# Instance norm of 268 MB on one core: tiles of 48 KiB per partition in four slots, masked sums, and the last stores on the load queue

## Chip, cores, metric

One core of one Trainium2 chip. The metric is the device time of one execution in microseconds; the span in a profile is about 1.7 us shorter. The engines go by the names of the profile: DVE is VectorE, ACT ScalarE, PE TensorE, POOL GpSimd, SP SyncE, which here only issues transfers. The transfers themselves are done by 16 DMA engines; a packet is what one of them moves as one record, here one row of one partition (the 63 whole loads of before, of 128 rows each, are 8,064 packets of 32 KiB) or a 4-byte write to a semaphore.

## The reference

```python
x = np.random.randn(8, 64, 32, 64, 64).astype(np.float32)   # 512 instances of 131072 elements
mean = np.mean(x, axis=(2, 3, 4), keepdims=True)
var = np.var(x, axis=(2, 3, 4), keepdims=True)
return ((x - mean) / np.sqrt(var + eps)).astype(np.float32)
```

268.4 MB are read once and 268.4 MB written once.

## The kernel before

A tile is 4 MB: 8 instances, 16 partitions each, 32 KiB per partition. Six slots (buffers in SBUF, the on-chip memory) hold tiles; SP issues loads, ACT issues stores. DVE and ACT share the sums and the final scaling, and TensorE averages over the partitions of an instance. The last tile is cut into two halves so that the compute after the last load is short.

```python
COLS = 8192
SLOTS = 6
...
def on_vector(eng, t, lane, n, c1, c2, c16):
    w = t.shape[1] // 2
    eng.reduce_sum(out=a[:, 0:1], in_=t[:, :w], ...)        # waits: landed
    ...
    eng.tensor_scalar(out=t[:, w:], ...)                    # (x * scale) + shift
def on_scalar(eng, t, lane, n, c1, c2, c16, dst):
    eng.activation(..., in_=t[:, w:], func=Act.Identity, accum_out=a[:, 1:2])
    eng.activation(..., in_=t, func=Act.Square, bias=a[:, 2:3], accum_out=a[:, 3:4])
    ...
    eng.activation(out=t[:, :w], ..., scale=a[:, 5:6], bias=a[:, 6:7])
    eng.dma_start(out=dst, in_=t)._wait_ge(done[lane], c2).then_inc(stored[lane], 16)
...
def load_all(eng):                                          # on SP
    for s in range(SLOTS):
        eng.dma_start(out=slots[s][:], in_=x_t[s]).then_inc(landed[s], 16)
    ...                                                     # then each load waits for its slot's store
```

## Time and profile before

| | before |
|---|---|
| time, median of the first three runs | 1248.04 us (1247.95 to 1248.22) |
| span of the profiled run | 1246.2 us |
| ACT, DVE busy | 79%, 38% |
| packets of the two data queues, share of 16 DMA engines | 99.9% |
| bytes over the span | 431 GB/s |

Read the queue shares first: they say whether the DMA engines have any time left. The lines are in the prediction below.

### The profile page before, as it was taken

The page shows a single profiled execution, that of the slowest core. Times are in us where ns is not written, and L with a number is a line of the kernel's source. Part 1 is how long each engine was busy: PE and PEld are TensorE (multiplying, and loading weights), DVE is VectorE, ACT ScalarE, POOL GpSimd, SP SyncE. Part 2 cuts the span into 40 slices and gives each one's busy share as a digit, 9 for nine tenths or more (in the row PEclk, how much of TensorE's full clock was granted, in tenths as well). Part 3 has the DMA queues.
Part 4 walks back from the last instruction along what each step waited for, and adds up shares of the span by engine and source line. Part 5 has one row for each costly group of instructions (what it writes and reads, how often), then busy time and mean ns, then how long its engine had stood idle before and what let it go on. Part 6 is the DMA issues. An engine that isn't in the chain of part 4 may idle for free.

```text
span 1246.2 us, 1808 instructions
## 1 busy us (share of the span) xinstructions
PE 76.4 (6%) x260; PEld 65.2 (5%) x260; DVE 468.0 (38%) x325; ACT 986.1 (79%) x410; POOL 1.9 (0%) x11
## 2 busy tenths in 40 slices
PE   0000000000000000000000000000000000000000
PEld 0000000000000000000000000000000000000000
DVE  2344334433334334343343433434334333343331
ACT  5888888887787878778777877787787778878774
POOL 0000000000000000000000000000000000000000
DMA  9999999999999999999999999999999999999998
GB/s 404 421 438 428 430 438 436 428 431 438 435 429 431 438 435 429 431 436 436 429 431 436 436 429 430 438 436 426 433 438 436 426 433 438 435 425 435 438 429 380
DMA packets 18722, 536.90 MB, mean 431 GB/s; under 512 B 2080, under 2 KB 2080, under 8 KB 2080
## 3 DMA queue, kind: packets, MB, share of 16 engines
q1 hardware_dynamic: 9360, 268.44, 50.0%
q10 hardware_dynamic: 9360, 268.44, 49.9%
q14 instruction: 2, 0.02, 0.0%
HBM read 268.44 MB, written 268.44 MB: 431 GB/s over the span
## 4 chain that ended last, share of the span: by engine, by line
ACT 48%; DVE 29%; another core or an unknown queue 13%; PE 6%; issue 1%; DMA 1%; ACTq 0%; DVEq 0%; SPq 0%
ACT unused L113 37%; DVE small L79 18%; DVE slot L95 8%; ACT slot L123 4%; ACT unused L107 4%; PE psum L136 3%; PE psum L143 3%; ACT small L120 1%; ACT L120 1%; DMA slot<-in_x_dram 1%; DVE small L89 1%; DVE small L82 1%; DVE small L92 1%; ACTq L130 0%
## 5 line engine op out<-in xcount | busy, mean ns | idle before, releaser
L113 ACT ACTIVATE unused<-slot,small 128x8192 uint8<-128x8192 f32 (+1 forms) x65 | 456.1, 7016 | 90.2 <-DVE small L82 90.2
L79 DVE TENSOR_REDUCE small<-slot 128x1 f32<-128x4096 f32 (+1 forms) x65 | 283.0, 4353 | 163.7 <-DMA slot<-in_x_dram 163.7
L107 ACT ACTIVATE unused<-slot 128x4096 uint8<-128x4096 f32 (+1 forms) x65 | 231.7, 3564 | 81.9 <-DMA slot<-in_x_dram 76.7
L123 ACT ACTIVATE slot<-slot,small 128x4096 f32<-128x4096 f32 (+1 forms) x65 | 243.7, 3749 | 27.6 <-DVE small L92 27.6
L89 DVE RECIPROCAL small<-small 128x1 f32<-128x1 f32 x65 | 10.6, 164 | 533.8 <-ACT small L120 533.8
L95 DVE TENSOR_SCALAR slot<-slot,small 128x4096 f32<-128x4096 f32 (+1 forms) x65 | 154.7, 2380 | 2.4
L136 PE MATMUL psum<-small,avg 128*128 128x2 f32 x130 | 38.2, 363 | 673.9 <-DVE small L79 548.5
L136 PEld LDWEIGHTS psum<-small,avg 128*128 128x128 f32 x130 | 32.6, 311 | 679.4 <-DVE small L79 552.7
L143 PE MATMUL psum<-small,avg 128*128 128x1 f32 x130 | 38.2, 363 | 480.6 <-ACT unused L113 480.6
L143 PEld LDWEIGHTS psum<-small,avg 128*128 128x128 f32 x130 | 32.7, 312 | 486.1 <-ACT unused L113 486.1
L120 ACT ACTIVATE small<-psum,eps_t 128x1 f32<-128x1 f32 x65 | 17.0, 261 | 37.4 <-PE psum L143 37.3
L82 DVE TENSOR_REDUCE small<-psum 128x1 f32<-128x2 f32 x65 | 10.4, 160 | 62.8 <-PE psum L136 62.8
L107 ACT ACT_TABLE_LOAD x10 | 12.8, 1283 | 10.4 <-ACT slot L123 7.1
L120 ACT ACT_TABLE_LOAD x10 | 12.8, 1283 | 0.2
L107 ACT ACTIVATION_READ_ACCUMULATOR unused<-slot 128x1 f32 x65 | 12.1, 186 | 0.0
L113 ACT ACTIVATION_READ_ACCUMULATOR unused<-slot,small 128x1 f32 x65 | 12.1, 186 | 0.0
L92 DVE TENSOR_TENSOR small<-small 128x1 f32<-128x1 f32 x65 | 10.4, 159 | 2.2
L204 POOL TENSOR_SCALAR_AFFINE_SELECT avg<-avg 128x128 f32<-128x128 f32 x4 | 1.3, 324 | 0.3
L201 POOL MEMSET avg<- 128x128 f32 x2 | 0.4, 204 | 0.5 <-SPq L42 0.5
L246 POOL MEMSET const-bfloat16-1.0<- 128x1 bf16 x1 | 0.1, 101 | 0.0
L246 POOL MEMSET const-uint8-127<- 128x1 uint8 x1 | 0.1, 101 | 0.0
L214 POOL MEMSET eps_t<- 128x1 f32 x1 | 0.1, 99 | 0.0
(2 smaller groups left out, 0.2 us busy)
## 6 DMA issues: line engine op xcount, KB each, us to landing
slot<-in_x_dram SPq DMA_DIRECT2D x63, 4096.0 KB, 53.3
out_dram<-slot ACTq DMA_DIRECT2D x63, 4096.0 KB, 45.3
slot<-in_x_dram SPq DMA_DIRECT2D x2, 2048.0 KB, 55.6
out_dram<-slot ACTq DMA_DIRECT2D x2, 2048.0 KB, 14.7
```

Source lines behind the costliest of these rows:

```text
L79: eng.reduce_sum(out=a[:, 0:1], in_=t[:, :w], axis=mybir.AxisListType.X)._wait_ge(landed[lane], c16).then_inc(summed[lane], 1)
L82: eng.tensor_reduce(out=a[:, 2:3], in_=psum[lane][:, 0:2], axis=mybir.AxisListType.X, op=Alu.add, negate=True,)._wait_ge(meaned[lane], c1) ...
L89: eng.reciprocal(out=a[:, 5:6], in_=a[:, 4:5])._wait_ge(rooted[lane], c1).then_inc(scaled[lane], 1)
L92: eng.tensor_mul(out=a[:, 6:7], in0=a[:, 2:3], in1=a[:, 5:6])._wait_ge(scaled[lane], c1).then_inc(shifted[lane], 1)
L95: eng.tensor_scalar(out=t[:, w:], in0=t[:, w:], scalar1=a[:, 5:6], scalar2=a[:, 6:7], op0=Alu.mult, op1=Alu.add,)._wait_ge(shifted[lane], ...
L107: eng.activation(out=unused[:, w : 2 * w], in_=t[:, w:], func=Act.Identity, accum_out=a[:, 1:2],)._wait_ge(landed[lane], c16).then_inc(sum ...
L113: eng.activation(out=unused[:, : 2 * w], in_=t, func=Act.Square, bias=a[:, 2:3], accum_out=a[:, 3:4],)._wait_ge(centred[lane], c1).then_in ...
L120: eng.activation(out=a[:, 4:5], in_=psum[lane][:, 2:3], func=Act.Sqrt, bias=eps_t[:, 0:1])._wait_ge(varied[lane], c1).then_inc(rooted[lane ...
L123: eng.activation(out=t[:, :w], in_=t[:, :w], func=Act.Identity, scale=a[:, 5:6], bias=a[:, 6:7],)._wait_ge(shifted[lane], c1).then_inc(don ...
L136: eng.matmul(out=psum[lane][:, 0:2], lhsT=avg[n][:], rhs=a[:, 0:2], start=True, stop=True,)._wait_ge(summed[lane], c2).then_inc(meaned[lan ...
L143: eng.matmul(out=psum[lane][:, 2:3], lhsT=avg[n][:], rhs=a[:, 3:4], start=True, stop=True,)._wait_ge(squared[lane], c1).then_inc(varied[la ...
L204: eng.affine_select(out=m[:], in_=m[:], pattern=[[sign * split, n], [0, split]], compare_op=Alu.is_ge, fill=0.0, base=0 if sign < 0 else s ...
```

## The change

Its intent: fewer and longer packets (48 KiB rows instead of 32 KiB), compute that starts after 2 MB instead of 4 MB, and an end in which the last stores come close behind the last loads. A tile of 6 MB holds 12 instances whose borders fall inside a partition's row, so sums are kept by chunk of 16 KiB and put together with masks. Two parts of 2 MB come first, 41 tiles follow, three parts of 2 MB end it. The last whole tile and these three parts are stored by SP, behind the last loads.

```diff
-    COLS = 8192
-    SLOTS = 6
+    CHUNK = 4096
+    THIRDS = 3
+    COLS = THIRDS * CHUNK
+    SLOTS = 4
+    FRONT = 2
+    n_tiles = (n_inst // PART - FRONT) // THIRDS - 1
+    n_parts = n_inst // PART - THIRDS * n_tiles
 ... (layout of tiles and parts, masks, semaphores)
+    def over_instance(eng, a, p, at, m, to, negate, c1, wait, steps):
+        eng.tensor_tensor(...)   # sums by chunk times mask
+        eng.tensor_reduce(...)   # of what TensorE averaged
+        eng.tensor_tensor(...)   # back to chunks
+        eng.tensor_reduce(...)
 ... (DVE squares chunk 0, ACT chunks 1 and 2; DVE scales 0 and 1, ACT 2)
+        for m in range(FRONT, n_parts):
+            part(m)                                   # last three loads
+        eng.dma_start(out=out_t[TAIL], in_=slots[s][:])._wait_ge(done[s], ...)
+        for m in range(FRONT, n_parts):
+            eng.dma_start(out=part_of(out_f, m), in_=t)._wait_ge(done[lane], 2)...
```

## The prediction

"Latencies some 3" is an estimate that the trace of before bears out: twice 1.02 us from the first issue (1.03) to the first packet (2.05) and 0.46 from the end of the last packet (1244.68) to the last landing (1245.14) are 3.0. The times of ACT and DVE that the compute per tile is worked out from are in the last fence.

> **What bounds the kernel now.** I read the page first (busy shares, DMA rows, queues), then the groups by shape, the waits of the engines and of the load queue, and the rates of three stretches.
>
> From the page:
>
> ```profile
> PE 76.4 (6%) x260; PEld 65.2 (5%) x260; DVE 468.0 (38%) x325; ACT 986.1 (79%) x410; POOL 1.9 (0%) x11
> ...
> DMA  9999999999999999999999999999999999999998
> ...
> DMA packets 18722, 536.90 MB, mean 431 GB/s; under 512 B 2080, under 2 KB 2080, under 8 KB 2080
> ...
> q1 hardware_dynamic: 9360, 268.44, 50.0%
> q10 hardware_dynamic: 9360, 268.44, 49.9%
> ...
> slot<-in_x_dram SPq DMA_DIRECT2D x63, 4096.0 KB, 53.3
> out_dram<-slot ACTq DMA_DIRECT2D x63, 4096.0 KB, 45.3
> ```
>
> The two queues' packets fill 99.9% of the time of all 16 DMA engines: there is no hole for better overlap to fill. A 4 MB load needs 53.3 us to land and a store 45.3 us, though 4.19 MB at 431 GB/s is 9.7 us: both queues always hold a backlog. ACT at 79% has room.
>
> The stretches (columns: PE, weight loads, DVE, ACT and POOL busy, clock, DMA share, GB/s) show start, middle and end:
>
> ```profile
> 0.00:3.00 3.00, 0.00 (x0) 0.00 (x0) 0.00 (x0) 0.00 (x0) 1.89 (x11) 1.00 0.65 175
> 3.00:1240.00 1237.00, 76.36 (x260) 65.23 (x260) 468.02 (x325) 986.06 (x410) 0.00 (x0) 1.00 1.00 433
> 1240.00:1246.20 6.20, 0.00 (x0) 0.00 (x0) 0.00 (x0) 0.00 (x0) 0.00 (x0) 1.00 0.43 182
> ```
>
> The middle runs at share 1.00 for 1237 us. What the edges lose is small: in the records of single packets the first data packet starts at 2.05 us and the last ends at 1244.68.
>
> The waits of the load queue and of DVE and ACT say the same:
>
> ```profile
> SPq L185 <- DMA out_dram<-slot: 1048.9, 54, 50.6
> ...
> DVE small L79 <- DMA slot<-in_x_dram: 163.7, 53, 13.2
> ...
> ACT unused L107 <- DMA slot<-in_x_dram: 76.7, 44, 8.6
> ```
>
> The load queue waits for stores to free slots, and the engines wait for loads. Both wait for the same DMA engines. The chain that ended last names ACT and DVE for most of the span; with the DMA always full I don't take it as the bound.
>
> [...] a 32 KiB packet takes 1213 ns, a 16 KiB one 611, a 4-byte semaphore write 9. Two 16 KiB packets are 9 ns longer than one of 32 KiB, so here the fixed cost is 9 ns and 16 KiB of data 602 ns. [...]
>
> ```profile
> L113 ACT ACTIVATE unused<-slot,small 128x8192 uint8<-128x8192 f32 x63 | 448.6, 7121 | 88.2 <-DVE small L82 88.2
> L79 DVE TENSOR_REDUCE small<-slot 128x1 f32<-128x4096 f32 x63 | 278.4, 4419 | 162.0 <-DMA slot<-in_x_dram 162.0
> L123 ACT ACTIVATE slot<-slot,small 128x4096 f32<-128x4096 f32 x63 | 239.5, 3801 | 26.8 <-DVE small L92 26.8
> L107 ACT ACTIVATE unused<-slot 128x4096 uint8<-128x4096 f32 x63 | 227.8, 3617 | 80.5 <-DMA slot<-in_x_dram 75.8 <-ACT slot L123 4.6
> L95 DVE TENSOR_SCALAR slot<-slot,small 128x4096 f32<-128x4096 f32 x63 | 152.0, 2413 | 2.3
> ...
> L113 ACT ACTIVATE unused<-slot,small 128x4096 uint8<-128x4096 f32 x2 | 7.4, 3707 | 2.0 <-DVE small L82 2.0
> ```
>
> **The change part by part.**
>
> *Packets.* Before, each of 16 engines moves, for 63 whole tiles and two halves, in both directions, 63 x 8 x 2 = 1008 packets of 32 KiB, 32 of 16 KiB and 130 semaphore writes: 1170 packets, 1008 x 1.213 + 32 x 0.611 + 130 x 0.009 = 1243.4 us. The packet records sum to 1244.9 us per engine; the other 1.5 us are slower packets, at the first loads (1.7 to 2.2 us each instead of 1.2) and near the first store at 34 us. After, there are 41 tiles of 6 MB and five parts of 2 MB: 41 x 8 x 2 = 656 packets of 48 KiB, 80 of 16 KiB and 92 semaphore writes, 828 in all. If a 48 KiB row goes as one packet, it takes 3 x 0.602 + 0.009 = 1.815 us: 1190.6 + 48.9 + 0.8 = 1240.3 us. The difference is 342 packets x 9 ns = 3.1 us, wholly on the bound.
>
> *Compute per tile.* First sums: DVE reduces 4096 and 1536 columns (4.42 and, interpolated with the 2.28 us of 2048 columns, 1.75), ACT sums 4096 and 2560 with accumulator reads of 0.19 (3.62 + 2.34 + 0.38 = 6.3). The masked mean adds to the old hop (0.9 us from sums to squares) one product ahead of the matmul and two small DVE steps after it, 0.2 each: 1.45. Squares: ACT twice (3.71 + 0.19) = 7.8; DVE beside it adds the mean (2.41)[...]. Masked variance, root, reciprocal, shift: 2.15. Last: DVE two scalings (2 x 2.41 = 4.85), ACT one (3.80), issue 0.4. Sum 6.3 + 1.45 + 7.8 + 2.15 + 4.85 + 0.4 = 23.0 us per tile. The DMA needs 2 x (8 x 1.815 + 0.009) = 29.1 us for the same tile. Before it was about 17.4 (spacing of the squares from 36.6 to 106 us) against 19.4. So compute gets relatively more room: 79% of the DMA's time instead of 90%. All of it lies beside the transfers.
>
> *Slots.* A slot's cycle is 4 x 29.1 = 116 us, as 6 x 19.4 was. Load and store at half rate each take 29.1, compute 23, latencies some 3: 84, which leaves 32 us of queueing (before about 60: 116 less 56). Less, but above zero, so both queues stay filled.
>
> *Start.* Two parts and tiles 0 and 1 (16.8 MB, 39 us of DMA) need no store first. Part 0 lands at about 8 us rather than 13.2, its store goes out at about 19 after 10.3 us (what the half tile takes at the end of before), lands near 31 and frees slot 2. The DMA is full from 2 us on in both kernels, so earlier compute is worth nothing.
>
> *End.* By the ledger of slots the last tile lands about 29 us before the last part, near 1178 and 1207 us. The tile's result is ready at 1178 + 23 = 1201, the parts' at 1212, 1222 and 1232. After 1207 only stores remain: 6.8 us of tile 39, 14.5 of tile 40, then 4.9 per part. Part 4's turn comes at about 1238, and it is ready with issue and first packet at 1234. So the engines don't run dry, with some 3 to 4 us to spare. Putting these stores on the load queue saves no transfer; it keeps ACT from standing at an issue while parts are to be computed.
>
> *Sum.* -3.1 us for packets, 0 for the rest: 1248.04 - 3.1 = 1244.9, rounded to 1245.0.
>
> **The rivals.** (a) The last stores starve. The margin of 3 us is an estimate[...]. Cost then 0 to 3 us: 1245 to 1248. For it: never measured here. Against: the ledger, and the backlog. (b) A 48 KiB row is cut in two packets. Then 1312 + 80 + 92 = 1484 packets, 314 more than before, +2.8 us: 1251. Against: 32 KiB goes as one packet now; I give it 6%. (c) Four slots are too few, or the chain nears 29 us; every DMA hole then adds its length to each round: 1255 and more. Against: 6 us of room per tile; 3%. (d) Shorter edges: two slower instruction packets and the first packets make one engine end 2 us behind the others before. A luckier end could give 1243.5 to 1244.
>
> **Range and chances.** The packet term is counted and its price measured, so the middle is narrow: 1245.0 us. Below, only (d): 1243.4. Above, (a) and small losses: 1247.6; (b) and (c) lie outside. [...] faster 0.01, within 2% 0.98, slower 0.01.
>
> **What would show it.** Packets about 13,250 instead of 18,722, queues together still near 100% of 16 engines, mean just over 432 GB/s, span near 1243.2. A single 48 KiB packet of 1.815 us would confirm the price; 24 KiB packets would show (b). Tile compute near 23 us from first sum to issue, with DVE near 65% and ACT near 63% busy (19.5 x 41 and 18.2 x 41 us plus the parts), would confirm the room; a DMA slice below 9 in the middle would show (c), and one in the last 10 us (a). Median landings should be some 45 us for loads and stores. The prediction is wrong if the rate inside packets itself changes with row length or layout, which no row of this profile speaks to.

## The result and the profile after

| | before | after |
|---|---|---|
| median of four runs | 1248.01 us (1247.95 to 1248.22) | 1248.11 us (1247.9 to 1251.57) |
| ratio of fast runs, 95% interval | | 1.0007 (0.999 to 1.0024) |
| span of the profiled run | 1246.2 us | 1246.2 us |

A ratio is the mean time of one kernel's fast runs over that of the other's fast runs of the same rounds, so it isn't quite the ratio of the medians. The time did not move: the predicted 3.1 us are missing, and 1248.11 lies above the range.

The page of the changed kernel, the lines that answer to those of before:

```profile
PE 55.0 (4%) x184; PEld 46.1 (4%) x184; DVE 804.6 (65%) x722; ACT 764.6 (61%) x441; POOL 2.7 (0%) x15
...
DMA packets 13250, 536.89 MB, mean 431 GB/s; under 512 B 1472, under 2 KB 1472, under 8 KB 1472
...
q1 hardware_dynamic: 7200, 281.02, 52.3%
q10 hardware_dynamic: 6048, 255.86, 47.4%
...
slot<-in_x_dram SPq DMA_DIRECT2D x41, 6144.0 KB, 39.9
out_dram<-slot ACTq DMA_DIRECT2D x40, 6144.0 KB, 54.2
```

The packets are as few as counted (13,250), and one of 48 KiB takes 1815 ns (the median of 10,496 in the trace). Yet the mean stays at 431 GB/s. The queues fill 99.7%. Loads and stores still wait in line, and by the waits the engines still idle for loads:

```profile
DVE small L159 <- DMA slot<-in_x_dram: 272.4, 39, 7.8
```

The difference is at the very end. The rates of stretches (the last two columns are the DMA share and GB/s), first of before, then of after:

```profile
1241.00:1242.00 1.00, 0.00 (x0) 0.00 (x0) 0.00 (x0) 0.00 (x0) 0.00 (x0) 1.00 0.99 426
1242.00:1243.00 1.00, 0.00 (x0) 0.00 (x0) 0.00 (x0) 0.00 (x0) 0.00 (x0) 1.00 0.69 295
1243.00:1244.00 1.00, 0.00 (x0) 0.00 (x0) 0.00 (x0) 0.00 (x0) 0.00 (x0) 1.00 0.04 16
```

```profile
1240.00:1241.00 1.00, 0.00 (x0) 0.00 (x0) 0.00 (x0) 0.00 (x0) 0.00 (x0) 1.00 1.07 459
1241.00:1242.00 1.00, 0.00 (x0) 0.00 (x0) 0.00 (x0) 0.00 (x0) 0.00 (x0) 1.00 0.39 164
1242.00:1243.00 1.00, 0.00 (x0) 0.00 (x0) 0.00 (x0) 0.00 (x0) 0.00 (x0) 1.00 0.31 131
1243.00:1244.00 1.00, 0.00 (x0) 0.00 (x0) 0.00 (x0) 0.00 (x0) 0.00 (x0) 1.00 0.31 131
```

Before, nearly all engines work until about 1243 us and then one alone (0.04 is less than 1/16). After, most have finished by about 1241.5, and a share of 0.31, five of sixteen, goes on until 1244. So most of the DMA engines did gain, and the end did not.

The trace shows it sharper. A DMA of these two kernels adds 1 to its semaphore 16 times (65 loads of before make 1,040 packets of 4 bytes on their queue). I take these as one for each of the 16 engines; the trace has the 16 times, without the name of the engine. For the last store of a kernel I take the first of them as the time when an undisturbed engine was through, and the time from the first to the last I call the lag. The end of the last store is read from the profiled run of each kernel:

| last store | first engine lands | lag of the last | last engine lands |
|---|---|---|---|
| before | 1243.05 | 2.09 (the next 0.78) | 1245.14 |
| after | 1241.56 | 3.33 (five engines 2.89 to 3.33, the next 0.44) | 1244.89 |

The first engine is 1.49 us earlier, the lag 1.24 us longer. These are the two questions: why 1.49 instead of 3.1, and where the lag comes from.

### The profile page after: what moved, and what is told of

It reads as the page before. It is cut to its first block, busy times and chain, and to the rows that moved or that the text cites. A ratio compares the mean times of both kernels' runs of the same rounds, so it can differ in the third digit from the quotient of the medians.

```text
span 1246.2 us, 1977 instructions
## 1 busy us (share of the span) xinstructions
PE 55.0 (4%) x184; PEld 46.1 (4%) x184; DVE 804.6 (65%) x722; ACT 764.6 (61%) x441; POOL 2.7 (0%) x15
## 2 busy tenths in 40 slices
DMA packets 13250, 536.89 MB, mean 431 GB/s; under 512 B 1472, under 2 KB 1472, under 8 KB 1472
## 4 chain that ended last, share of the span: by engine, by line
another core or an unknown queue 82%; DMA 9%; ACT 3%; DVE 2%; SPq 1%; issue 1%; PE 0%; ACTq 0%
DMA slot<-in_x_dram 6%; DMA out_dram<-slot 4%; ACT unused L222 1%; SPq L391 1%; ACT unused L292 1%; DVE small L159 0%; ACT unused L215 0%; DVE slot L202 0%; DVE slot L195 0%; ACT slot L302 0%; PE psum L253 0%; DVE small L266 0%; ACT unused L289 0%; PE psum L316 0%
## 5 line engine op out<-in xcount | busy, mean ns | idle before, releaser
L215 ACT ACTIVATE unused<-slot 128x4096 uint8<-128x4096 f32 x82 | 243.5, 2970 | 302.4 <-DMA slot<-in_x_dram 300.1
L159 DVE TENSOR_REDUCE small<-slot 128x1 f32<-128x4096 f32 x82 | 249.2, 3081 | 272.4 <-DMA slot<-in_x_dram 272.4
L222 ACT ACTIVATE unused<-slot,small 128x4096 uint8<-128x4096 f32 x82 | 303.5, 3703 | 63.6 <-DVE small L145 63.6
L173 DVE CUSTOM_DVE_ANT_0 unused<-slot 128x4096 uint8<-128x4096 f32 x41 | 181.5, 4426 | 1.4
L235 ACT ACTIVATE slot<-slot,small 128x4096 f32<-128x4096 f32 x41 | 155.9, 3802 | 18.1 <-DVE small L190 18.1
L202 DVE TENSOR_SCALAR slot<-slot,small 128x4096 f32<-128x4096 f32 x41 | 98.7, 2408 | 0.0
L253 PE MATMUL psum<-small,avg 128*128 128x9 f32 (+1 forms) x164 | 49.1, 375 | 1116.5 <-DVE small L127 1116.5
L166 DVE TENSOR_SCALAR slot<-slot,small 128x4096 f32<-128x4096 f32 x41 | 96.5, 2353 | 1.5
L195 DVE TENSOR_SCALAR slot<-slot,small 128x4096 f32<-128x4096 f32 x41 | 96.3, 2348 | 0.0
L253 PEld LDWEIGHTS psum<-small,avg 128*128 128x128 f32 x164 | 41.1, 311 | 1124.5 <-DVE small L127 1124.5
L133 DVE TENSOR_REDUCE small<-psum 128x3 f32<-128x12 f32 x82 | 13.9, 169 | 56.6 <-PE psum L253 56.6
L292 ACT ACTIVATE unused<-slot,small 128x4096 uint8<-128x4096 f32 x5 | 18.5, 3709 | 6.0 <-DVE small L269 6.0
L139 DVE TENSOR_TENSOR small<-small,belongs 128x9 f32<-128x9 f32 x82 | 14.0, 170 | 2.8
## 6 DMA issues: line engine op xcount, KB each, us to landing
slot<-in_x_dram SPq DMA_DIRECT2D x41, 6144.0 KB, 39.9
out_dram<-slot ACTq DMA_DIRECT2D x40, 6144.0 KB, 54.2
out_dram<-slot SPq DMA_DIRECT2D x3, 2048.0 KB, 19.5
```

The lines of the kernel that those rows point to most:

```text
L139: eng.tensor_tensor(out=block(a, by_chunk, n, n), in0=spread(a, by_instance, n), in1=belongs[:, :, :n].rearrange("p i c -> p c i"), op=Alu ...
L159: eng.reduce_sum(out=column(a, SUMS, j), in_=part, axis=AXIS)._wait_ge(landed[lane], c16).then_inc(summed[lane], 1)
L166: eng.tensor_scalar(out=chunk[0], in0=chunk[0], scalar1=column(a, MEANS, 0), scalar2=None, op0=Alu.add,)._wait_ge(centred[lane], c1).then_ ...
L173: eng.tensor_tensor_reduce(out=unused[2][:], in0=chunk[0], in1=chunk[0], scale=1.0, scalar=0.0, op0=Alu.mult, op1=Alu.add, accum_out=colum ...
L195: eng.tensor_scalar(out=chunk[0], in0=chunk[0], scalar1=column(a, SCALES, 0), scalar2=None, op0=Alu.mult,)._wait_ge(scaled[lane], c1).then ...
L202: eng.tensor_scalar(out=chunk[1], in0=chunk[1], scalar1=column(a, SCALES, 1), scalar2=column(a, SHIFTS, 1), op0=Alu.mult, op1=Alu.add,)._w ...
```

## The experiments

**Theory.** The DMA engines alone set the time. A packet costs about 4.8 ns and not 9, and the end is set by the slowest of 16 engines, whose lag grew. **Rivals.** Compute slows the transfers; or the lag is a chance event of one run; or the new place of the last stores made it; or something else than the slowest engine sets the end. Each kernel ran in five rounds against before, the first of them profiled, whose medians in the three calls of several kernels were 1248.09 to 1248.13 us and in the last, of one, 1247.98. Each call ran on another chip, with before beside it.

| run | median, range (us) | first engine lands the last store | lag |
|---|---|---|---|
| repeat | 1248.25 (1248.12 to 1248.65) | 1241.50 | 3.61 |
| tail_back | 1253.38 (1253.04 to 1256.94) | 1250.22 | 0.15 |
| copy32 | 1247.6 (1246.69 to 1247.62) | 1244.25 | 0.57 |
| copy48 | 1247.19 (1245.14 to 1247.63) | 1241.59 | 2.67 |
| copy16 | 1254.15 (1254.03 to 1254.26) | 1250.34 | 0.89 |
| paced48 | 1248.0 (1247.83 to 1251.45) | 1241.48 | 6.97 |
| paced_short | 1248.58 (1247.34 to 1251.32) | 1241.62 | 2.72 |
| no_tail_parts | 1247.85 (1247.71 to 1249.88) | 1243.39 | 1.47 |
| front_off | 1248.96 (1247.78 to 1251.56) | 1241.83 | 2.93 |
| before_tail | 1248.0 (1247.94 to 1248.19) | 1243.02 | 2.09 |
| skip15 | 1251.44 (1251.33 to 1251.74) | 1243.09 (two DMAs) | 5.51 |
| pieces | 1247.11 (1246.9 to 1249.4) | 1243.78 | 2.64 |

Where the last store was issued only after the engines had run out of other work (copy16, copy32, no_tail_parts, tail_back, pieces), they start it nearly together, so most of these lags are short (0.15 to 1.47 us, in pieces 2.64) and the first landings late; they are not to be compared with the rest. The two right columns are of the profiled run, which for paced48 (1251.45) and pieces (1249.4) is the slowest of the five. All outputs passed the comparison. That says nothing for the kernels that only copy: the drawn inputs have a mean near 0 and a variance near 1, so the unnormalised input passes too.

### repeat: the same kernel again

No edit. 

> The changed kernel again, unaltered. Theory A (the lag of single DMA engines is set by the program): the profile shows the same picture as the first one, 11 engines landing the last store within 0.5 us of each other, five of them 2.9 to 3.3 us after the first, and a median of 1248.0 to 1248.2 us. Theory B (the slow packets near 264 and 1185 to 1214 us are chance events of one run): the spread of the last landing differs by more than 1 us from 3.3 us and the times scatter by about as much.

The picture came again: four engines 2.87 to 3.61 us after the first, the next 0.74, and slow packets at the same moments (1184.7 to 1185.9, 1204.5 to 1205.4, 1212.1 to 1213.7 us). The median is 1248.25, just above the 1248.0 to 1248.2 of theory A, and the runs scatter by 0.5 us. Theory A holds for the most part; the number of late engines (four, not five) and single slow packets differ.

### copy32, copy48, copy16: the transfers alone

```diff
-    (sums, squares, root and scaling on DVE, ACT and TensorE)
-        eng.dma_start(out=dst, in_=t)._wait_ge(done[lane], c2)...
+        eng.dma_start(out=dst, in_=t)._wait_ge(landed[lane], c16)...
 copy16 besides:
-    COLS = 8192
-    SLOTS = 6
+    COLS = 4096
+    SLOTS = 12
```

> Only the transfers of the kernel before (32 KiB rows, six slots): every store waits for its load alone, nothing is computed, the output is wrong on purpose. Theory A (the DMA engines alone set the time): 1248.0 us within 0.5, although all compute is gone. Rival (compute holds transfers up somewhere, or its reads and writes slow packets): 1245 us or less.

> Only the transfers of the changed kernel (48 KiB rows, four slots, parts at both ends, last stores on the load queue), wrong output on purpose. If the price of a packet is 4.8 ns, as the rounds of 116.174 and 116.000 us say, and the lag of five engines comes from the transfers themselves, 1248 us within 0.5. If the lag comes from compute beside the transfers (instruction fetches included), the last landing has a spread below 1 us and the time is 1246.0 to 1246.7, 1.6 us under copy32's fast engines. With 9 ns a packet it would be 3.1 us under copy32.

> Only transfers, with 16 KiB rows and twelve slots. A round of 24 MB both ways has 192 data packets and 24 semaphore writes per engine instead of 96 and 12: with 4.8 ns a packet it takes 116.174 + 108 x 0.0048 = 116.69 us on the engines that don't lag; with 9 ns 117.15 us. Whole kernel about 1252 us with the first price, 1257 with the second.

With all compute gone copy32 is 0.5 us faster than before by the medians and copy48 0.9, neither clear of the noise (ratios 0.9993 with 0.9979 to 1.0006, and 0.9989 with 0.9975 to 1.0003): the DMA engines set the time, as the prediction had it. copy48's expectation was hit by neither branch cleanly: there is no slow packet at its end, but one engine still lands 2.67 us late and the median is 1247.19. Its stretches (POOL busy, clock, DMA share, GB/s):

```profile
1241.00:1242.00 1.00, 0.00 (x0) 1.00 0.20 82
1242.00:1243.00 1.00, 0.00 (x0) 1.00 0.08 33
1243.00:1244.00 1.00, 0.00 (x0) 1.00 0.04 16
```

Here one engine is late (0.04), where the full kernel has five (0.31). So one laggard comes with the bare transfers, the other four with something that this copy lacks: the compute, or the pace that it gives the transfers.

The three tilings give the price of a packet. In the middle of the run the first engine's landings of one slot come in steady steps, each a round of 24 MB in and out:

| rows | data packets and semaphore writes per engine and round | round (us) |
|---|---|---|
| 16 KiB (copy16) | 192 + 24 | 116.696 |
| 32 KiB (before; copy32 the same within 0.01) | 96 + 12 | 116.174 |
| 48 KiB (after, copy48) | 64 + 8 | 116.000 |

(116.696 - 116.174) / 108 and (116.174 - 116.000) / 36 are both 4.83 ns. I had predicted 116.69 for copy16 with 4.8 ns and 117.15 with 9. (Its whole time, 1254.15 us, lies 2 us above the 1252 expected with the first; the rest is outside the steady rounds and was not followed up.) The 9 ns came from the recorded durations, but packets of one engine overlap a little in the records: 96 x 1.213 + 12 x 0.009 = 116.56 us of duration pass in 116.174. The starts of successive packets of one engine say the same: 607 ns apart at 16 KiB, 1209 to 1210 at 32 and 1811 to 1812 at 48, each 3 to 4 ns less than the recorded 611, 1213 and 1815; after a semaphore write the next starts in 6 ns. Two spacings at 16 KiB are thus some 4 to 5 ns longer than one at 32. This settles what the rounds leave open, since all three tilings have eight data packets to one semaphore write: the data packets themselves have this price, and not only the write. Carried on to no packets at all, the round would be 115.65 us for 50.33 MB, some 435 GB/s (an estimate, extrapolated from the three rounds of the table).

So the change can gain 342 x 4.83 ns = 1.65 us, and the first engine's landing shows 1.49.

### tail_back: the last stores on ACT's queue

```diff
-            if with_target and k == TAIL:
-                more = (None,)
-        (SP's stores of the last tile and of the three parts)
+        (ACT stores them as all others)
```

> The changed kernel with the last whole tile and the last three parts stored on ACT's queue, as all others. If the new place of the last stores brings the slow packets after 1185 us (1.0 to 1.5 us on five engines), the last landing comes about 1 us earlier: 1247.0 us, spread 2.0 to 2.4 us. If those slow packets come from the part loads with their 16 KiB rows, or from lag that was there before, the time stays at 1248.1 within 0.3 us. If the move keeps ACT free and that matters, it gets slower than 1248.5.

It is 5.1 us slower than the changed kernel in the same rounds (1253.38 against 1248.25), and the DMA engines run dry. The stretches of tail_back (PE, weight loads, DVE, ACT, POOL, clock, DMA share, GB/s):

```profile
1232.00:1240.00 8.00, 0.59 (x2) 0.50 (x2) 2.45 (x2) 5.18 (x3) 0.00 (x0) 1.00 0.63 268
1240.00:1250.00 10.00, 0.59 (x2) 0.50 (x2) 1.67 (x3) 2.97 (x4) 0.00 (x0) 1.00 0.50 211
```

and in its instructions in order of time ACT stands waiting for the last two part loads:

```profile
1216.66 1.91 ACT L289 ACTIVATE unused<-slot 128x2048 uint8<-128x2048 f32 x1 [7.24 <-DMA slot<-in_x_dram]
...
1233.66 1.91 ACT L289 ACTIVATE unused<-slot 128x2048 uint8<-128x2048 f32 x1 [6.58 <-DMA slot<-in_x_dram]
```

In the changed kernel the last part lands at 1215.8 us, here at 1233.6. The trace shows the two queues taking turns row by row: while the first end part loads in the changed kernel, most of its 16 KiB packets (86 of 113 looked at) are followed 0.607 us later by one of 48 KiB, and the next of 16 KiB starts 2.42 us after the last. Beside a queue of 48 KiB packets, eight packets of 16 KiB should take 8 x (0.611 + 1.815) = 19.4 us. The first end part takes just that in both kernels (1176.7 to 1196.1 in the changed one), the second 20.2 us in tail_back. So a load of 16 KiB rows gets a quarter of the bytes, not half, as long as stores of 48 KiB rows stand in the other queue: from 1176.7 to 1196.1 us the packets of the changed kernel bring 2.10 MB in and 6.29 MB out. With the last tile's store behind the loads on the same queue, the store queue empties at 1208.3, and the last part has the engines to itself. That is what this piece of the change is for: it keeps the new tiling from losing 5 us at its end. None of the three outcomes was this one: the third had the time (above 1248.5 us), but gave a freer ACT as the reason. And a rival falls: tail_back still has slow packets after 1170 us, 27 of them by over 40 ns, some 0.4 us per engine in all, so they don't need the new place of the last stores.

### before_tail: this part of the change alone

```diff
+        (SP, behind the last loads: stores of the last whole tile and of both halves)
-        (the same three on ACT)
```

> One part of the change alone, on the kernel before: the last whole tile and both halves are stored on the load queue, in its 32 KiB tiling and six slots. If the order of the last stores costs or gains something only where 16 KiB loads meet 48 KiB stores, it does nothing here: 1247.8 to 1248.4 us. If the load queue is a better place for the last stores as such, 1 us or more less; if a store there waits for what stands ahead of it, more.

1248.0 us, landing 1243.02, lag 2.09: nothing, as expected where no long store packets stand beside the last short loads for long.

### no_tail_parts: only whole tiles at the end

```diff
-    n_tiles = (n_inst // PART - FRONT) // THIRDS - 1
+    n_tiles = (n_inst // PART - FRONT) // THIRDS
```

> The changed kernel with 42 whole tiles behind the two front parts and no part at the end. Compute of the last tile then starts when the last load lands, so I expect the DMA engines to run dry before the last store: last load near 1211 us, store issued 22 us later with one tile of stores in between (14.5 us), so 6 to 10 us late: 1252 to 1257 us. What it is for: if the slow packets after 1185 us come from the part loads beside 48 KiB stores, they are gone here (under 0.1 us per engine until the last load has landed).

Two answers. The time is 1247.85, not 1252 to 1257: two tiles of stores are left when the last load has landed at 1205.7, they last until 1229.4, and the last tile is ready just about then. I had counted one. And the slow packets are gone: from 1170 us on, one packet was slowed by more than 40 ns, at 1228.9 us when the loads were long done. In the changed kernel there are 20 between 1185 and 1214.3, by 6.2 us in all, and by the landings they fell on the engines that then land late: the five longest lags go from 1.4 to 2.4 us at 1177 to 2.9 to 3.3 at 1216, while the others stay below 0.5. So the second part of the lag is made where the part loads stand beside the stores of whole tiles. That is a place and not yet a cause: copy48 has the same end parts without a slow packet, and front_off, with two end parts, has three.

### paced48 and paced_short: the transfers at the kernel's pace, with no engine at the slots

```diff
+    pace_in, pace_out = two halves of PSUM, [P, 2048] fp32 each
-        (sums, squares, root and scaling on DVE, ACT and TensorE)
-            eng.dma_start(out=dst, in_=t)._wait_ge(done[lane], c3)
+        (11 activations pace_out <- pace_in per tile, 5 per part)
+            eng.dma_start(out=dst, in_=t)._wait_ge(done[lane], c1)
 paced_short: ten of the eleven in an inner loop, so the program is shorter
```

> The changed kernel's transfers at its own pace: between landing and store of a tile ACT runs 11 activations of 2048 columns from one half of PSUM to the other (some 21 us; five for a part, some 10), and no engine touches the slots. Output wrong on purpose. Theory A (the lag comes from the order and the pace of the transfers: the 16 KiB part loads beside 48 KiB stores, then a stretch of loads only): slow packets after 1185 us of about 0.4 us per engine, last landing spread 2.8 to 3.6 us, 1248 us. Theory B (ACT's and DVE's reads and writes of SBUF slow single packets): no packets slowed by over 40 ns after 1170 us, spread 2 to 2.7 us, 1246.5 to 1247.2 us as in the bare copy.

> The paced transfers again (48 KiB rows, 11 PSUM activations per tile, no engine at the slots), but the activations of a tile in a small inner loop, so that the program is short and no instruction fetch should fall among the transfers. Theory P (pace and order of the transfers make the lag): slow packets between 45 and 1170 us of 0.3 us or more per engine again, last landing spread 3 us or more, 1247.8 us and up. Theory F (an instruction fetch sets one engine back and the rest follows from it): with no fetch, under 0.2 us per engine as in the bare copy, spread under 2.8 us, 1247.3 us or less. In both the first engine should land the last store near 1241.5 us.

Both have slow packets after 1170 us, 0.31 and 0.27 us per engine, like the changed kernel's 0.40, and unlike copy48's 0.01 (all time above the median packet of each size, summed). No engine read or wrote the slots. So the slow packets at the end don't need DVE or ACT at the slots; the order and pace of the transfers suffice. Theory A of paced48 stands for the end.

paced48 shows more. Its five runs fall into two groups, 1247.83 to 1248.0 and 1251.38 and 1251.45, and the profile caught a slow one. Its first engine lands at 1241.48 as in the other 48 KiB kernels with three end parts whose engines don't run dry, but one engine lags by 6.97 us. Against the profiled run of the changed kernel the time is 3.55 us longer (1251.45 and 1247.90) and the lag 3.64. The time follows the lag of one engine to a tenth of a microsecond. The single slow run of the changed kernel (1251.57) has no profile; that it is the same is likely, not shown.

paced_short did not do what it was built for: one instruction fetch of 8 KiB still fell among its transfers, at 131.9 us. Its slow packets in the middle (0.27 us per engine) lie between the two branches, and its lag of 2.72 fits the second, its median of 1248.58 the first. Whether an instruction fetch starts the lag in the middle stays open.

### front_off: no parts at the front

```diff
-    FRONT = 2
+    FRONT = 0        (and 42 whole tiles, two parts at the end)
```

> The changed kernel without the two parts at the front: 42 tiles from the first, two parts at the end. First compute starts near 17 instead of 8.8 us. If an early start is worth nothing because the DMA engines are full anyway, within 1 us of the changed kernel (1247.5 to 1248.6); if the start counts, up to 8 us more.

The profiled run took 1247.78 us, the median is 1248.96 with a scatter of 3.8 us. The first engine lands at 1241.83, 0.3 us after the changed kernel's: an early start of compute is worth at most that on this engine. The median missed the expected window by 0.4 us; it is not clear of the noise (ratio to before 1.0012, 0.9998 to 1.0025). Here only one engine is really late, by 2.93 us, the next by 1.34, with three slow packets after 1170 us, 0.8 us in all; yet the profiled run took as long as the changed kernel's. One late engine is enough to set the end.

### skip15: take work from one engine

```diff
+        if lane == LANES - 1:
+            for rows in (slice(0, 120), slice(120, 128)):
+                eng.dma_start(out=dst[rows], in_=t[rows])...
```

> The kernel before, whose last store (2 MB) is cut in two: rows 0 to 119[...] and rows 120 to 127[...]. Theory (the end is set by the one engine that lags 2.1 us; the other 15 end within 0.8 us): if the laggard is the engine left out, the last landing comes near 1244.2 instead of 1245.1 us[...]: 1247.1 us. If the laggard is another engine, [...] 1248.1 to 1248.7. If the lag of one engine doesn't set the end at all, 1248.1 to 1248.7 too, but then the landings of the last store show no single late one.

It failed as a test. Packets of this last store took up to 2.2 us instead of 0.61, most of the slowed ones about 1.2: 1.73 us more per engine. Why, no run shows. How the two stores are spread over the engines was the author's assumption; the times given rested on it. The profile has 2,087 packets under 512 B where before has 2,080, so by this count the two together write 23 times to their semaphore instead of 16: the spread did change, but that one engine was left out is not shown. The run cannot tell which engine lags.

### pieces: the last tile stored by chunks, without end parts

```diff
 (on no_tail_parts)
-        eng.dma_start(out=out_t[TAIL], in_=slots[s][:])._wait_ge(done[s], ...)
+        for i in (0, 2, 1):
+            cols = slice(i * CHUNK, (i + 1) * CHUNK)
+            eng.dma_start(out=out_t[TAIL][:, cols], in_=slots[s][:, cols])._wait_ge(piece[i], 1)...
```

> The 42 whole tiles without parts at the end, with the last tile stored by chunks as each is ready, first of them 2.4 us earlier than the whole. In the run without this 15 engines landed the last store within 0.16 us of each other, which I read as all of them having waited for it, about 1 us for the slowest. If so, 1246.6 to 1247.2 us, under both kernels, and the last landings spread again by over 1.5 us. If the DMA engines did not wait there, 1247.8 to 1248.2 as before it.

Four runs of five lie between 1246.9 and 1247.31, the fifth at 1249.4; the median is 1247.11, 1.0 us under before of the same rounds (1248.09). The ratio of 0.9992 (0.9978 to 1.0006) does not clear the noise. The median fits the first branch of the expectation. The profile fell on the run of 1249.4, so it does not show what the good runs did; in it an engine was already 5.1 us behind at 1208 us. This is the best full kernel by its median, and its gain of less than a tenth of a per cent is not shown.

## Why the prediction was wrong, and where it was right

**Right: the bound.** The DMA engines set the time, with or without compute (copy32 1247.6 us, before beside it 1248.13), and the change gained far less than 2%. By the estimate from the rounds, some 435 GB/s, even no packets at all would leave 1234 us for the 536.87 MB, 1.1% less than before.

**Right: the compute.** The tile from landing to issue took 21.9 us (1176.73 to 1198.62 us) where 23.0 was worked out. DVE is at 65% as foreseen, ACT at 61% (63 foreseen). The multiply-and-sum of 4096 columns took 4426 ns, as long as the reduction of before (4419); the estimate for it, which no trace had shown, is cut above. Its row beside that of a scaling:

```profile
L173 DVE CUSTOM_DVE_ANT_0 unused<-slot 128x4096 uint8<-128x4096 f32 x41 | 181.5, 4426 | 1.4
...
L202 DVE TENSOR_SCALAR slot<-slot,small 128x4096 f32<-128x4096 f32 x41 | 98.7, 2408 | 0.0
```

**Right: packets and start.** 48 KiB rows go as single packets (10,496 of 49,152 bytes in the trace), so rival (b) fell; rivals (a) and (c), that transfers starve, did not happen either (the DMA share is 1.00 from 3 to 1240 us). The early start was worth 0.3 us at most on the first engine (front_off).

**Wrong: "The difference is 342 packets x 9 ns = 3.1 us, wholly on the bound".** This term was mis-sized. A packet costs 4.83 ns and the term 1.65 us. The profile of before already spoke against 9: I noted 1244.9 us of packets per engine and that all of them lie between 2.05 and 1244.68 us. 1244.9 us of work in 1242.6 us of time means overlap, and durations that overlap don't add up to time.

**Wrong: taking the mean of 16 engines for the end.** "-3.1 us for packets, 0 for the rest" set the edges equal. Rival (d) had seen an engine end 2 us behind the others, and only as something that could get shorter. It put this down to two instruction packets and the first packets, but in before the lag grows by 0.18 us in each round from some 300 us on. It got longer: 3.33 us instead of 2.09. So 1.49 us were gained on the first engine and 1.24 lost in lag, and the remaining quarter of a microsecond is within the scatter of runs. The lag has at least two sources. One engine falls behind in both kernels: in before the last engine needs 116.35 us for a round and the others 116.17, and in the changed kernel one loses 0.23 us a round from 275 us on. A late engine needs neither compute nor an instruction fetch: copy48 has neither (13,248 packets and no instruction queue in its profile), and one engine lands the last store 2.67 us after the first. And slow packets hit engines that already lag, in the middle and above all from 1185 to 1214 us; no_tail_parts shows that the second stretch goes with the end parts, tail_back that it does not need the new place of the stores, the paced copies that no engine at the slots is needed. At 1174 us, before that stretch, the longest lag was 2.38 us, so most of the growth over before's 2.09 was made after it.

**Wrong: the ledger of the end.** It had the parts land by 1207 us at half rate; they landed at 1215.8, as their 16 KiB packets take turns with packets of 48 KiB. "Putting these stores on the load queue saves no transfer" named the wrong use: without it the changed kernel takes 5.1 us more. The landings of whole tiles (45 us for both foreseen) are 39.9 for loads and 54.2 for stores; the sum fits, the split does not.

**Open.** What slows the packets: all these engines work at full share, and no row of a profile says what holds one of them up. Why front_off and copy48 are nearly free of them at the end. Which engine drifts. What starts the lag before 300 us, where instruction fetches and single slow packets coincide in some runs.

## What to carry to other kernels

Take the price of a packet from the spacing of packets, not from their recorded length: on these full DMA engines it was 4.83 ns and not 9, and 342 packets fewer were worth 1.65 us (an estimate from that price) and not 3.1. Look at the spread of the 16 landings of the last store: here the end was that of the slowest DMA engine, and of the 1.49 us that the first engine gained, 1.24 were lost in a lag of 3.33 us instead of 2.09. And where short rows and long rows stand in two queues at once, look at who gets the bytes: 16 KiB rows beside 48 KiB rows got a quarter here, 19.4 us for 2.1 MB instead of some 4.9 (an estimate, 8 x 0.611), and the last stores left in the other queue cost 5.1 us. So put what must land soon where no long packets stand beside it.
